# Rotating block-made queries and keys: halves swapped by ScalarE copies and three whole VectorE operations, and a slot of its own for the sample tile's keys

## The chip, the cores and the metric

The kernel runs on one core of one Trainium2 chip. The metric is the time of one execution on the device in microseconds (us), as a median over runs. A core has engines that run side by side, each through its own list of instructions in order: TensorE (PE; loads of stationary operands are shown apart as PEld), VectorE (DVE), ScalarE (ACT), GpSimd (POOL) and SyncE (SP), which issues the transfers (DMA). An instruction may wait for a semaphore of another engine or transfer; then everything behind it on its engine waits too. Tiles live in on-chip memory (SBUF, 128 partitions) or in the accumulators of TensorE (PSUM).

## The reference, cut to what matters

One layer over a prompt of 2048 frames and 8 running streams of 16 new frames each. The input projection makes retention queries and keys (4 heads of 128), their values and gates, and sliding-window queries (8 heads of 64), keys and values (2 heads). Queries and keys are rotated:

```
def rope(x, pos, rot_dim, theta):
    ...
    xr = x[..., :rot_dim].astype(jnp.float32)
    x1, x2 = xr[..., :half], xr[..., half:]
    rot = jnp.concatenate([x1 * cos - x2 * sin, x2 * cos + x1 * sin], axis=-1).astype(x.dtype)
    return jnp.concatenate([rot, x[..., rot_dim:]], axis=-1)

def in_proj(x, pos, w_in):
    ...
    rq = rope(rq.reshape(b, t, RET_HEADS, RET_DK), pos, RET_DK, RET_THETA)
    rk = rope(rk.reshape(b, t, RET_HEADS, RET_DK) * (RET_DK ** -0.5), pos, RET_DK, RET_THETA)
    ...
    sq = rope(sq.reshape(b, t, SWA_HEADS, SWA_HD), pos, SWA_ROT_DIM, SWA_THETA)
    sk = rope(sk.reshape(b, t, SWA_KV_HEADS, SWA_HD), pos, SWA_ROT_DIM, SWA_THETA)
```

For retention the whole head of 128 is rotated, in halves of 64; for the sliding window only the first 16 of 64. Then come chunkwise retention and banded attention with sinks, an output projection, layer norm, an MLP (1024 to 4096 to 1024, squared ReLU) and a second layer norm. The sliding-window keys of the last 128 prompt frames and of the 128 new frames are outputs as well.

## The kernel before, in words

The 2176 frames are 17 tiles of 128: 0 to 15 are the prompt, 16 (`SAMPLE`) holds the new frames of the eight streams. They are worked through in three groups, `[0..4]`, `[5..10]` and `[16, 11..15]`. A group passes through stages, whose names stand in the tile names of the profile: `1kv` is keys and values of the sliding window in group 1 (counted from 0), `1qk` retention queries and keys, `1sq` sliding-window queries and their attention, `1ret` retention, `1out` the output projection, `1mlp` the MLP.

The order of the instructions on each engine is fixed when the program is built. A planner (`Sched`) keeps a modelled clock for each engine; side work is written as tasks (Python generators) that yield the modelled time at which they want to go on. Between each three matmuls (`mm3`) the planner lets those tasks run whose time has come (`S.pump`); where TensorE needs a result, `finish` and `S.until` run tasks until it is there. `idle()` holds a task back while VectorE's modelled backlog is over 1 us. So an operation that is modelled shorter, or put on another engine, moves others around it. Transfers are all issued by SyncE in the order in which the tasks ask for them (but for a few on GpSimd).

Tiles come from pools by tag, with a fixed number of slots: `y` has 20, `u3` 8, `xT` 14, `st` 2, and in PSUM `mm` 2, `rt` 2, `sw` 4. `take` gives out the slot that was freed first, and what writes it first waits for the last reader of its former tile, be that an engine or a transfer.

In groups 1 and 2 the retention queries and keys are made by blocks: for each head h seven products (`QK`: 11, 12, S2, S1, S4, S3, 22) of 12 matmuls of 384 frames each stand in for eight (`qk_units`). S3 and 22 of a head share a PSUM bank. ScalarE copies products to `y` tiles of 128x384 (`keep`, `direct`), VectorE adds others to them from PSUM (`plus`); TensorE can only start product 22 of a head when `plus` has read S3 of it. A finished block, transposed (dimension on the partitions, frames along the row), goes to `rope_task`, which multiplies it by a table of cosines and sines and leaves it in `xT`. There are 16 blocks a group: 4 heads, queries and keys (u), two halves of the group's frames (v). The table of a half v (`table`, 384 KB, in a `u3` slot) is loaded when the first block asks for it. In the profile a rotation reads `xT_2qk<-y_2qk,u_2qk` for the halves, `y_2qk<-y_2qk,u_2qk` for the cosine and `xT_2qk<-xT_2qk,y_2qk` for the sum, all in line 310, the helper `vtt`; line 294 is ScalarE's copy (`acopy`), 316 a fused operation of VectorE (`vstt`), 275 a matmul, 281 a transpose on TensorE, 356 a transfer's issue.

The sliding-window keys of a tile (`kv_task`) are copied from PSUM by ScalarE into a tile of the pool `y` (groups 1 and 2), rotated by a few small VectorE operations (`rope_small`), for tiles 15 and 16 written out by a transfer, and transposed by TensorE. `sq_task` does the like for queries.

Of the kernel before, what the change touches and what calls it, by code (L numbers as in the profile page):

```python
# [11 lines left out]
ALU = mybir.AluOpType  # L12
AX = mybir.AxisListType

P = 128
# [3 lines left out]
SAMPLE = 16  # L19
# [157 lines left out]
def tile_layer(ctx: ExitStack, tc: tile.TileContext, A: dict, O: dict):  # L177
# [6 lines left out]
    S = Sched()  # L184
# [10 lines left out]
    def room(tag, n=1):  # L195
        return live[tag] + n <= CAP[tag]
# [5 lines left out]
    def take(tag, shape, dt=F32):  # L202
        if not room(tag):
            assert not S.inside, f"no room in {tag}"
            S.until(lambda: room(tag))
        live[tag] += 1
        cnt[0] += 1
        t = (psp if tag in PS else sb).tile(shape, dt, tag=tag, bufs=CAP[tag], name=f"{tag}_{ph[0]}_{cnt[0]}")
        name = t.tensor.name if hasattr(t, "tensor") else t.name
        tag_of[name] = tag  # L210
        S.fence[name] = min(freed[tag])
        freed[tag].remove(S.fence[name])
        return t
# [18 lines left out]
    def drop(*tiles):  # L232
        for t in tiles:
            name = t.tensor.name if hasattr(t, "tensor") else t.name
            mine = [u for u in lent if u.tensor.name == name]
            if mine:
                i = (t.offset % DM) // 512
                spare_blocks.append(mine[0][:, 512 * i:512 * i + 512])
                continue
            tag = tag_of.pop(name)  # L240
            live[tag] -= 1
            freed[tag].append(S.last(name) + S.ALIEN)
            for tab in (S.wr, S.rd):
                tab.pop(name, None)

    def wait_room(tag, n=1):
        while not room(tag, n):
            yield S.now + 0.3
# [6 lines left out]
    def size(ap):  # L255
        n = 1
        for d in ap.shape[1:]:
            n *= d
        return n
# [18 lines left out]
    def transpose(out, in_):  # L278
        cost = 0.110 + (0.2 if S.parts != (False, False) else 0.0)
        S.parts = (False, False)  # L280
        S.run("PE", lambda: nc.tensor.transpose(out, in_, ident), [out], [in_], cost)
# [11 lines left out]
    def acopy(out, in_):  # L293
        S.run("ACT", lambda: nc.scalar.copy(out, in_), [out], [in_], 0.06 + 0.83e-3 * size(out))  # L294

    def dcost(out):
        return 0.067 + 1.04e-3 * size(out)
# [4 lines left out]
    def copy(out, in_):  # L302

        n = size(out)
        ta = S.start_of("ACT", [out], [in_]) + 0.06 + 0.83e-3 * n
        tv = S.start_of("DVE", [out], [in_]) + dcost(out) + 0.3
        (acopy if ta <= tv else vcopy)(out, in_)

    def vtt(out, a, b, op):
        S.run("DVE", lambda: nc.vector.tensor_tensor(out, a, b, op), [out], [a, b], dcost(out))  # L310
# [37 lines left out]
    def dma(out, in_):  # L348
        t = S.start_of("SP", [out], [in_])
        S.free["SP"] = t + 0.06  # L350
        on_chip = out if hasattr(out.tensor, "slot_key") else in_
        nbytes = on_chip.shape[0] * size(on_chip) * 4
        end = max(S.free["DMA"], t + 1.1) + nbytes / 359e3
        S.free["DMA"] = end
        S.note("DMA", [out], [in_], end + 1.0)
        nc.sync.dma_start(out=out, in_=in_)
# [455 lines left out]
    def idle(eng="DVE", slack=SLACK):  # L812
        while S.free[eng] > S.now + slack:
            yield S.now + 0.2
# [238 lines left out]
    def rope_small(x, nh, t, ab):  # L1053

        c = cst[:, C_RS + 16 * t:C_RS + 16 * t + 8]
        s = cst[:, C_RS + 16 * t + 8:C_RS + 16 * t + 16]
        xv = x[:, :, 0:16].rearrange("p h (u f) -> p h u f", u=2)
        a = ab[:, 0:16 * nh].rearrange("p (h u f) -> p h u f", u=2, f=8)
        b = ab[:, 16 * nh:32 * nh].rearrange("p (h u f) -> p h u f", u=2, f=8)
        vtt(a, xv, c.unsqueeze(1).unsqueeze(1).broadcast_to([P, nh, 2, 8]), ALU.mult)  # L1060
        vtt(b, xv, s.unsqueeze(1).unsqueeze(1).broadcast_to([P, nh, 2, 8]), ALU.mult)
        vtt(xv[:, :, 0, :], a[:, :, 0, :], b[:, :, 1, :], ALU.subtract)
        vtt(xv[:, :, 1, :], a[:, :, 1, :], b[:, :, 0, :], ALU.add)

    def kv_task(t, si, ps, kTall, vall):
        tag = "y" if ph[0][0] != "0" else "xT"
        yield from wait_room(tag)
        kb = take(tag, [P, 256])
        krf = kb[:, 0:P]
        kr = krf.rearrange("p (g d) -> p g d", g=2)  # L1070
        acopy(krf, ps[:, 0:P])
        acopy(vall[:, si, :], ps[:, P:2 * P])
        drop(ps)
        yield S.ready(krf, eng="DVE")
        rope_small(kr, 2, t, kb[:, P:2 * P])
        if t >= NT - 2:
            nm = "p" if t == NT - 2 else "s"
            yield S.ready(krf, eng="SP")
            dma(O["swa_k_" + nm], krf)
            dma(O["swa_v_" + nm], vall[:, si, :])  # L1080
        yield S.soon(krf, more={'0': 0.0}.get(ph[0][0], 3.0))
        yield from wait_room("rt")
        tp = take("rt", [P, P])
        transpose(tp, krf)
        drop(kb)
        copy(kTall[:, (si) * P:(si + 1) * P], tp)
        drop(tp)
# [730 lines left out]
    for gi, tiles in enumerate(GROUPS):  # L1818
# [12 lines left out]
        def table(v):  # L1831
            while v not in tables:
                yield from wait_room("u3")
                if v in tables:
                    break
                tables[v] = t = take("u3", [P, 2, 384])
                dma(t, A["ropeT"][gi - 1, v])
                tabled[v] = 0
            return tables[v]
# [3 lines left out]
        def rope_task(c, h, u, v):  # L1843

            tab = yield from table(v)
            if h not in qkT:
                while h not in qkT and not room("xT"):
                    yield S.now + 0.3
                if h not in qkT:
                    qkT[h] = take("xT", [P, 1536])  # L1850
            dst = qkT[h][:, 768 * u + 384 * v:768 * u + 384 * v + 384]
            yield S.ready(c, tab, eng="DVE")
            yield from idle()
            vtt(dst[0:64], c[64:128], tab[64:128, 1, :], ALU.mult)
            vtt(dst[64:128], c[0:64], tab[0:64, 1, :], ALU.mult)
            yield from idle()
            vtt(c, c, tab[:, 0, :], ALU.mult)
            vtt(dst, dst, c, ALU.add)
            drop(c)
            tabled[v] += 1  # L1860
            if tabled[v] == 2 * RH:
                drop(tables[v])

        def qk_units(gi):

            def rope(c, h, u, v):
                rope_tasks[h, v].append(S.add(rope_task(c, h, u, v)))
# [105 lines left out]
        if gi:  # L1973
            T, used, qkT = {}, {}, {}
# [6 lines left out]
        for tis, kts in [(a, [0]), (a, [1]), (a, [2]), (a, [3]), (b, [0, 1, 2, 3]), (a, [4, 5]), (a, [6, 7]),  # L1981
# [9 lines left out]
            for ti in tis:  # L1991
# [3 lines left out]
                for kt in kts:  # L1995
                    o = P * (ti % 3)
                    xh, xl = x_at(gi, ti // 3, kt, slice(o, o + P))
                    c = (kt % 4) * 256
# [110 lines left out]
        for ui, u in enumerate(units):  # L2109
            nh, ti = u  # L2110
            t = tiles[ti]
# [406 lines left out]
```

## Time and profile before

| what | value |
|---|---|
| median of 3 runs | 2274.81 us (2274.16 to 2275.93) |
| profiled execution, its own time | 2276.4 us |
| its span (first to last instruction) | 2274.6 us |
| granted TensorE clock, mean | 0.997 of full |
| busy: PE, PEld, DVE, ACT, POOL | 2245.1, 1978.4, 1616.5, 925.7, 73.3 us |

How the lines are read that follow. A row of a timeline has the start (us from the start of the span), the duration, the engine, the source line, the operation, what it writes and reads by the program's names, the shape, how many are put together (x), and in brackets how long the engine had stood idle before it and what ended that. SPq is SyncE's own queue: a transfer's issue, not the transfer. A row of the waits has the waiting instruction, the releaser, us in total, times, the longest. A row of windows has the stretch, its length, then busy time and instructions of each engine, the granted clock, the busy share of the transfer engines and GB/s. A row of groups has busy us, mean ns of one, then the idle time ahead of it and what ended it.

### The profile page before, as it was taken

Reading aid. Unit: us, or ns where it says so; the run is one execution under the profiler, and the core shown is the slowest. Engines: PE = TensorE matmul, PEld = TensorE weight load, DVE = VectorE, ACT = ScalarE, POOL = GpSimd, SP = SyncE. Lnnn points to the kernel's source line nnn. Section 1 sums busy time; section 2 is a strip of 40 time slices with the busy share of each in tenths; the row PEclk is TensorE's granted clock in tenths of the full one; section 3 lists DMA queues with packets and bytes.
Section 4 is the critical chain, followed back from the end, with each engine's and each line's share of the span. In section 5 each row is a group of like instructions: output and inputs, shape, how many; then the busy total and the mean of one; then the engine's idle time right before and its main releaser. Section 6 shows DMA issues by size and latency. Waiting matters only on the chain. (4 is left out here: it accounts for less than half of the span.)

```text
span 2274.6 us, 34114 instructions
## 1 busy us (share of the span) xinstructions
PE 2245.1 (99%) x12185; PEld 1978.4 (87%) x12185; DVE 1616.5 (71%) x3472; ACT 925.7 (41%) x2205; POOL 73.3 (3%) x104
## 2 busy tenths in 40 slices
PE   9999999999999999999999999999999999999998
PEld 7788899998889878889989899898778899999987
DVE  6766788788878877788766666798654865555557
ACT  5534644444454255474233333252433732222222
POOL 0000000000000000000000000000010000000002
PEclk9999999999999999999999999999999999999999
DMA  7646746787899767759999999984344577777776
GB/s 277 210 167 230 274 177 236 262 287 277 280 335 376 241 231 254 270 189 359 360 374 368 372 353 357 347 311 183 129 138 166 175 251 258 252 256 252 250 257 180
DMA packets 205976, 598.34 MB, mean 263 GB/s; under 512 B 21872, under 2 KB 54384, under 8 KB 205808
## 3 DMA queue, kind: packets, MB, share of 16 engines
q1 hardware_dynamic: 204512, 593.81, 72.7%
q0 software_dynamic: 1296, 2.36, 0.6%
q8 instruction: 96, 1.57, 0.3%
q14 instruction: 72, 0.59, 0.1%
HBM read 422.48 MB, written 171.18 MB: 261 GB/s over the span
## 5 line engine op out<-in xcount | busy, mean ns | idle before, releaser
L275 PE MATMUL sw_2mlp<-xT_2out,w_2mlp 128*128 128x384 f32 x1152 | 209.0, 335 | 0.3 <-DVE kvln_2mlp L310 0.3
L275 PE MATMUL sw_1mlp<-xT_1out,w_1mlp 128*128 128x384 f32 x1152 | 209.1, 335 | 0.0
L275 PEld LDWEIGHTS sw_2mlp<-xT_2out,w_2mlp 128*128 128x128 f32 x1152 | 202.1, 188 | 4.2 <-DVE kvln_2mlp L310 0.6
L275 PEld LDWEIGHTS sw_1mlp<-xT_1out,w_1mlp 128*128 128x128 f32 x1152 | 202.3, 188 | 3.7
L275 PE MATMUL sw_0mlp<-xT_0out,w_0mlp 128*128 128x320 f32 x1188 | 180.2, 309 | 1.8 <-ACT y_0mlp L294 1.4
L275 PEld LDWEIGHTS sw_0mlp<-xT_0out,w_0mlp 128*128 128x128 f32 x1188 | 176.5, 188 | 5.0 <-ACT y_0mlp L294 1.8
L275 PE MATMUL rt_1mlp<-w_1mlp,u_1mlp 128*128 128x512 f32 x516 | 127.3, 391 | 1.2 <-DMA w_1mlp<-keptd 1.1
L275 PE MATMUL rt_2mlp<-w_2mlp,u_2mlp 128*128 128x512 f32 (+1 forms) x522 | 127.1, 388 | 0.0
L275 PE MATMUL rt_0mlp<-w_0mlp,u_0mlp 128*128 128x512 f32 x492 | 122.5, 394 | 1.6 <-ACT w_0mlp L294 0.8
L275 PE MATMUL mm_2mlp<-w_2mlp,u_2mlp 128*128 128x512 f32 (+1 forms) x504 | 122.5, 388 | 0.0
L275 PE MATMUL mm_1mlp<-w_1mlp,u_1mlp 128*128 128x512 f32 x492 | 121.6, 391 | 0.8 <-DMA w_1mlp<-keptd 0.8
L275 PEld LDWEIGHTS rt_1mlp<-w_1mlp,u_1mlp 128*128 128x128 f32 x516 | 96.3, 188 | 21.2 <-DMA w_1mlp<-keptd 2.2
L275 PEld LDWEIGHTS rt_2mlp<-w_2mlp,u_2mlp 128*128 128x128 f32 x522 | 96.9, 188 | 19.0
L275 PE MATMUL mm_0mlp<-w_0mlp,u_0mlp 128*128 128x512 f32 x456 | 111.6, 390 | 1.7 <-ACT w_0mlp L294 0.9
L275 PEld LDWEIGHTS rt_0mlp<-w_0mlp,u_0mlp 128*128 128x128 f32 x492 | 92.6, 190 | 21.3 <-DVE w_0mlp L310 1.3
L275 PEld LDWEIGHTS mm_2mlp<-w_2mlp,u_2mlp 128*128 128x128 f32 x504 | 93.6, 188 | 18.4
L275 PEld LDWEIGHTS mm_1mlp<-w_1mlp,u_1mlp 128*128 128x128 f32 x492 | 91.8, 188 | 19.5 <-DMA w_1mlp<-keptd 1.4
L275 PEld LDWEIGHTS mm_0mlp<-w_0mlp,u_0mlp 128*128 128x128 f32 x456 | 85.0, 188 | 19.4 <-ACT w_0mlp L294 1.4
L310 DVE TENSOR_TENSOR w_0mlp<-raw_0mlp,w_0mlp 128x512 fp32r<-128x512 f32 (+1 forms) x70 | 64.7, 925 | 44.7 <-ACT w_0mlp L294 30.4
L310 DVE TENSOR_TENSOR w_1mlp<-w_1mlp,w_1mlp 128x512 fp32r<-128x512 f32 (+1 forms) x100 | 67.2, 687 | 20.5 <-ACT w_1mlp L294 15.4
L294 ACT CAST u_2mlp<-kvln_2mlp 128x384 fp32r<-128x384 f32 x51 | 26.2, 515 | 117.7 <-PE mm_2mlp L275 44.1
L294 ACT CAST w_1mlp<-w_1mlp 128x512 fp32r<-128x512 f32 x70 | 43.4, 620 | 71.8 <-PE sw_1mlp L275 24.1
(974 smaller groups left out, 4713.5 us busy)
## 6 DMA issues: line engine op xcount, KB each, us to landing
w_1mlp<-keptd SPq DMA_DIRECT2D x112, 512.0 KB, 7.1
w_1mlp<-kept SPq DMA_DIRECT2D x104, 512.0 KB, 6.0
w_2mlp<-kept SPq DMA_DIRECT2D x104, 512.0 KB, 4.0
w_2mlp<-keptd SPq DMA_DIRECT2D x98, 512.0 KB, 4.1
kept<-w_0mlp SPq DMA_DIRECT2D x96, 512.0 KB, 3.4
keptd<-w_1mlp SPq DMA_DIRECT2D x70, 512.0 KB, 6.1
raw_0mlp<-in_wdn_dram SPq DMA_DIRECT2D x31, 512.0 KB, 5.9
keptq<-y_0mlp SPq DMA_DIRECT2D x56, 256.0 KB, 3.7
```

The costliest lines, as they stand in the source:

```text
L275: S.run("PE", lambda: nc.tensor.matmul(out, lhsT, rhs, start=start, stop=stop, skip_group_check=again), [out], [lhsT, rhs], cost)
L294: S.run("ACT", lambda: nc.scalar.copy(out, in_), [out], [in_], 0.06 + 0.83e-3 * size(out))
L310: S.run("DVE", lambda: nc.vector.tensor_tensor(out, a, b, op), [out], [a, b], dcost(out))
```

## The change

A rotation was four VectorE operations: the two halves of 64 partitions each multiplied crosswise (upper half of the block by sine into the lower half of the result, and the reverse), the block by cosine, and the sum. Now ScalarE copies the halves crosswise into the result, and VectorE does three operations on all 128 partitions: block by cosine, result by sine, sum. The sign that belongs to the sine moves with it to the other half of the table, which the host lays out. The task now waits for its place in `xT` and for the block on ScalarE ahead of the copies, and holds back for VectorE's backlog only ahead of the multiplications (one `idle()` after the table, one ahead of the sum).

The second edit: the sample tile's keys are taken from the pool `st` where it has room, and else from `y` as before; the others stay.

```diff
     def kv_task(t, si, ps, kTall, vall):
         tag = "y" if ph[0][0] != "0" else "xT"
-        yield from wait_room(tag)
-        kb = take(tag, [P, 256])
+        while not room(tag) and not (t == SAMPLE and room("st")):
+            yield S.now + 0.3
+        kb = take("st" if t == SAMPLE and room("st") else tag, [P, 256])
...
             dst = qkT[h][:, 768 * u + 384 * v:768 * u + 384 * v + 384]
-            yield S.ready(c, tab, eng="DVE")
-            yield from idle()
-            vtt(dst[0:64], c[64:128], tab[64:128, 1, :], ALU.mult)
-            vtt(dst[64:128], c[0:64], tab[0:64, 1, :], ALU.mult)
+            yield max(S.ready(c, eng="ACT"), S.fence[qkT[h].tensor.name])
+            acopy(dst[0:64], c[64:128])
+            acopy(dst[64:128], c[0:64])
+            yield S.ready(c, tab, dst, eng="DVE")
             yield from idle()
             vtt(c, c, tab[:, 0, :], ALU.mult)
+            vtt(dst, dst, tab[:, 1, :], ALU.mult)
+            yield from idle()
             vtt(dst, dst, c, ALU.add)
...
-    ropeT = np.concatenate([rt, rt * np.array([1.0, -1.0], np.float32)[:, None]], 2)
+    ropeT = np.concatenate([rt * np.array([1.0, -1.0], np.float32)[:, None], rt], 2)
```

The order of instructions differs from stage `1qk` to `1out` and from `2kv` to `2out`; the rest of the program stands as it was. VectorE has 36 instructions fewer (64 halves, 32 wholes more, and 4 copies less), ScalarE 68 more (64 copies of halves, and 4 copies which the planner moved there); TensorE has the same ones. Three places follow. A number behind a name only tells tiles apart; `DMAHW...` in a wait is a transfer's semaphore.

ScalarE in the stage `2kv` before: between the squares for the layer norm of group 1 stand the copies of keys out of PSUM.

```order
L290 ACTIVATE y_2kv_15428,tiny_2kv_15387<-y_1out_10492,tiny_2kv_15386 128x512 [waits Activation_49]
L294 COPY y_2kv_15464<-sw_2kv_15409 128x128 [waits DMAHW4_49,PE_49]
L294 COPY kvln_2kv_15372<-sw_2kv_15409 128x128
L294 COPY kvln_2kv_15371<-rt_2kv_15510 128x128 [waits PE_49]
L290 ACTIVATE y_2kv_15495,tiny_2kv_15457<-y_1out_10405,tiny_2kv_15456 128x512 [waits DVE_49]
```

After, the same place:

```order
L290 ACTIVATE y_2kv_15445,tiny_2kv_15404<-y_1out_10509,tiny_2kv_15403 128x512 [waits Activation_49]
L294 COPY y_2kv_15481<-sw_2kv_15426 128x128 [waits PE_49]
L294 COPY kvln_2kv_15389<-sw_2kv_15426 128x128
L294 COPY kvln_2kv_15388<-rt_2kv_15527 128x128 [waits PE_49]
L290 ACTIVATE y_2kv_15488,tiny_2kv_15439<-y_1out_10310,tiny_2kv_15438 128x512 [waits DVE_49]
```

The copies stand in the same order; the first no longer waits for a transfer.

VectorE in the stage `2qk` before, from the last output sums of group 1 (line 316) to the second `plus` behind the second table (`u_2qk_15997` is that table, `mm_2qk_16047` and `mm_2qk_16070` are S3 of heads 0 and 1).

```order
L316 SCALAR_TENSOR_TENSOR y_1out_10797<-y_1out_10797,tiny_2qk_15871,y_1mlp_15269 128x512 [waits DVE_49]
L310 TENSOR_TENSOR xT_2qk_15723<-y_2qk_15995,u_2qk_15997 64x384 [waits DMAHW6_49,Activation_49]
L310 TENSOR_TENSOR xT_2qk_15723<-y_2qk_15995,u_2qk_15997 64x384
L310 TENSOR_TENSOR y_2qk_15995<-y_2qk_15995,u_2qk_15997 128x384 [waits DMAHW7_49,DVE_49]
L310 TENSOR_TENSOR xT_2qk_15723<-xT_2qk_15723,y_2qk_15995 128x384 [waits DVE_49]
L310 TENSOR_TENSOR xT_2qk_15752<-y_2qk_16017,u_2qk_15997 64x384 [waits Activation_49]
L310 TENSOR_TENSOR xT_2qk_15752<-y_2qk_16017,u_2qk_15997 64x384
L310 TENSOR_TENSOR y_2qk_15911<-y_2qk_15911,mm_2qk_16047 128x384 [waits DMAHW1_49,PE_49]
L310 TENSOR_TENSOR y_2qk_16017<-y_2qk_16017,u_2qk_15997 128x384 [waits DMAHW1_49,DVE_49]
L310 TENSOR_TENSOR xT_2qk_15752<-xT_2qk_15752,y_2qk_16017 128x384 [waits DVE_49]
L310 TENSOR_TENSOR y_2qk_15929<-y_2qk_15929,mm_2qk_16070 128x384 [waits PE_49]
```

After (`u_2qk_16023` is the table, `mm_2qk_16074` and `mm_2qk_16095` are S3 of heads 0 and 1):

```order
L316 SCALAR_TENSOR_TENSOR y_1out_10814<-y_1out_10814,tiny_2qk_15890,y_1mlp_15286 128x512 [waits DVE_49]
L310 TENSOR_TENSOR y_2qk_15934<-y_2qk_15934,mm_2qk_16074 128x384 [waits PE_49]
L310 TENSOR_TENSOR y_2qk_16021<-y_2qk_16021,u_2qk_16023 128x384 [waits DMAHW1_49,DMAHW0_49,Activation_49]
L310 TENSOR_TENSOR xT_2qk_15740<-xT_2qk_15740,u_2qk_16023 128x384
L310 TENSOR_TENSOR xT_2qk_15740<-xT_2qk_15740,y_2qk_16021 128x384 [waits DVE_49]
L310 TENSOR_TENSOR y_2qk_16044<-y_2qk_16044,u_2qk_16023 128x384 [waits Activation_49]
L310 TENSOR_TENSOR xT_2qk_15771<-xT_2qk_15771,u_2qk_16023 128x384
L310 TENSOR_TENSOR xT_2qk_15771<-xT_2qk_15771,y_2qk_16044 128x384 [waits DVE_49]
L310 TENSOR_TENSOR y_2qk_15954<-y_2qk_15954,mm_2qk_16095 128x384 [waits DMAHW2_49,PE_49]
```

`plus` of head 0 moved from behind the first use of the table to ahead of it; `plus` of head 1 now stands behind two whole rotations. On SyncE's queue the table's load stands behind two more stores of output tiles than before.

VectorE in the stage `1sq` before, from the first rotation of sliding-window queries (`xT_1sq` and `u_1sq`) on; `st_1sq`, `raw_1sq` are parts of weights.

```order
L310 TENSOR_TENSOR xT_1sq_8526<-u_1sq_8510,cst 128x128 [waits Activation_49]
...
L310 TENSOR_TENSOR raw_1sq_8469<-raw_1sq_8470,raw_1sq_8469 128x512 [waits DVE_49]
L310 TENSOR_TENSOR xT_1qk_8056<-y_1qk_8120,u_1qk_8037 64x384 x2
L310 TENSOR_TENSOR y_1qk_8120<-y_1qk_8120,u_1qk_8037 128x384 [waits DVE_49]
L310 TENSOR_TENSOR xT_1qk_8056<-xT_1qk_8056,y_1qk_8120 128x384 [waits DVE_49]
L310 TENSOR_TENSOR y_1qk_8136<-y_1qk_8136,u_1qk_8037 128x384
L310 TENSOR_TENSOR xT_1qk_8073<-xT_1qk_8073,y_1qk_8136 128x384 [waits DVE_49]
L310 TENSOR_TENSOR xT_1sq_8579<-u_1sq_8561,cst 128x128 [waits Activation_49]
```

After:

```order
L310 TENSOR_TENSOR xT_1qk_8095<-xT_1qk_8095,y_1qk_8171 128x384 [waits DVE_49]
L310 TENSOR_TENSOR xT_1sq_8552<-u_1sq_8539,cst 128x128 [waits Activation_49]
...
L310 TENSOR_TENSOR raw_1sq_8494<-raw_1sq_8495,raw_1sq_8494 128x512 [waits DVE_49]
L310 TENSOR_TENSOR raw_1sq_8583<-raw_1sq_8494,raw_1sq_8583 128x512 [waits Activation_49]
L310 TENSOR_TENSOR xT_1sq_8606<-u_1sq_8590,cst 128x128 [waits Activation_49]
```

All rotations of retention blocks now stand ahead of the first of the sliding-window queries.

## The prediction, made before the changed kernel had run

> **What bounds the kernel now.** I read the page's busy times first, then TensorE's waits over the whole span, then busy times by stage, and last the instructions around each wait.
>
> ```profile
> span 2274.6 us, 34114 instructions
> PE 2245.1 (99%) x12185; PEld 1978.4 (87%) x12185; DVE 1616.5 (71%) x3472; ACT 925.7 (41%) x2205; POOL 73.3 (3%) x104
> ```
>
> TensorE (PE) is busy for 2245.1 of 2274.6 us. No edit touches a matmul, so all that can be won lies in the 29.5 us in which it stands still, and in what its clock loses. VectorE (DVE) at 71% is no bound over the span; it can be one only in a stage. The view of waits, TensorE alone, the rows that fall in the stages whose order the change moves:
>
> ```profile
> PE mm_2qk L275 <- DVE y_2qk L310: 2.2, 1, 2.2
> PE rt_2qk L281 <- ACT kvln_2kv L294: 1.9, 1, 1.9
> PE rt_2ret L275 <- DMA u_2ret<-in_st_dram: 1.6, 1, 1.6
> PE sw_1sq L275 <- ACT y_1sq L294: 1.6, 1, 1.6
> PE sw_1sq L281 <- DVE u_1sq L310: 1.5, 2, 1.3
> PE rt_2sq L281 <- DVE u_2sq L310: 1.3, 2, 0.7
> ```
>
> Columns: total, times, longest. These six make 10.1 us. That is the whole stock for a change that shortens VectorE's work here, plus what the clock loses. The busy times by stage (PE, PEld, DVE, ACT, POOL, granted clock, DMA) show how tight VectorE is there: group 1's queries and keys, then its sliding-window queries, then group 2's keys, and its queries and keys:
>
> ```profile
> 715.00:775.00 60.00, 60.00 (x343) 59.26 (x342) 41.97 (x72) 14.82 (x27) 0.00 (x0) 1.00 0.92 325
> 775.00:830.00 55.00, 51.55 (x296) 40.43 (x295) 46.03 (x118) 28.19 (x89) 0.00 (x0) 1.00 0.62 236
> 1480.00:1500.00 20.00, 18.12 (x134) 17.76 (x134) 15.88 (x52) 12.83 (x44) 1.10 (x2) 1.00 0.99 374
> 1500.00:1560.00 60.00, 57.83 (x319) 56.73 (x318) 56.54 (x109) 20.74 (x47) 3.58 (x4) 0.97 0.88 325
> ```
>
> In 1500 to 1560 VectorE is busy for 56.54 of 60 us, as full as TensorE, and ScalarE (ACT) for 20.74. That is the stage where fewer VectorE operations count, and the only one of the four with a clock under 1.00.
>
> **Part 1: the sample tile's keys in their own slot.** The timeline at the key-and-value stage of group 2:
>
> ```profile
> 1494.61 0.27 ACT L294 COPY y_2kv<-sw_2kv 128x128 f32<-128x128 f32 x1 [6.31 <-DMA out_swa_k_s_dram<-y_2kv]
> 1494.91 0.30 DVE L310 TENSOR_TENSOR y_2kv<-y_2kv,cst 128x32 f32<-128x32 f32 x2 [2.19 <-ACT y_2kv L294]
> 1498.85 0.33 PE L281 MATMUL rt_2qk<-cst,y_2kv 128*128 128x128 f32 x1 [1.88 <-ACT kvln_2kv L294]
> ```
>
> ScalarE's next key copy goes into the slot from which the sample keys are being written out, and stands 6.31 us for that transfer. What is queued behind it (two copies, two squares with their sums, more key copies) comes late, and TensorE's transpose waits 1.88 us for one of those copies. In the new order the copy waits for its matmul alone. Gain: 1.9 us at most. At least 0: if a square's inputs (VectorE's 2.19 us of waiting ends with this copy, not before it) were as late anyway. I take 1.9, since all of ScalarE's backlog there is this one wait. The change takes no room from anything: the other keys keep their tiles.
>
> **Part 2: the price of a rotation.** The rows around the second table of group 2 (start, duration):
>
> ```profile
> 1533.97 0.45 SPq L356 DMA_DIRECT2D u_2qk<-in_ropeT_dram  x1
> 1541.63 1.12 DVE L310 TENSOR_TENSOR xT_2qk<-y_2qk,u_2qk 64x384 f32<-64x384 f32 x2 [1.92 <-DMA u_2qk<-in_ropeT_dram]
> 1542.79 0.56 DVE L310 TENSOR_TENSOR y_2qk<-y_2qk,u_2qk 128x384 f32<-128x384 f32 x1
> 1543.95 1.12 DVE L310 TENSOR_TENSOR xT_2qk<-y_2qk,u_2qk 64x384 f32<-64x384 f32 x2
> 1545.11 0.56 DVE L310 TENSOR_TENSOR y_2qk<-y_2qk,mm_2qk 128x384 f32<-128x384 f32 x1
> 1545.58 0.55 DVE L310 TENSOR_TENSOR y_2qk<-y_2qk,u_2qk 128x384 f32<-128x384 f32 x1
> 1545.72 5.99 PE L275 MATMUL mm_2qk<-xT_2qk,w_2qk 128*128 128x384 f32 x24 [2.17 <-DVE y_2qk L310]
> 1546.16 0.56 DVE L310 TENSOR_TENSOR xT_2qk<-xT_2qk,y_2qk 128x384 f32<-128x384 f32 x1
> 1551.55 4.32 PE L275 MATMUL rt_2qk<-xT_2qk,w_2qk 128*128 128x384 f32 x24
> ```
>
> One rotation takes 1543.95 − 1541.63 = 2.32 us: two half operations that cost as much as whole ones, and two whole ones. Whole operations start 0.47 us apart where the second does not need the first (1545.11 to 1545.58) and 0.58 where it does (1545.58 to 1546.16). Three whole ones therefore take between 0.47 + 0.58 + 0.47 = 1.53 and 3 × 0.58 = 1.74 us; I take 1.64, the middle, so 0.68 us less for each, 11 us in each group of 16.
>
> The Trainium skill (VectorE: DVE Perf Modes, section "Two Vector instructions with no wait between them") says that an instruction starting in another group of 32 partitions than the input or output before it is held until all earlier ones have finished. By that rule the crossing halves could never overlap and the whole ones can: 1.53, and 13 us in a group; the trace agrees for the halves, with 1.12 us for two.
>
> The two copies go to ScalarE. No row shows one of 64x384; the nearest are these, by operation:
>
> ```profile
> L294 ACT COPY y_2qk<-sw_2qk 128x384 f32<-128x384 f32 x16 | 7.7, 481 | 15.3 <-DMA out_y_dram<-y_1out 8.3 <-DMA out_y_dram<-y_1ret 2.8 <-PE sw_2qk L275 2.6
> L294 ACT CAST u_2mlp<-kvln_2mlp 128x384 fp32r<-128x384 f32 x51 | 26.2, 515 | 117.7 <-PE mm_2mlp L275 44.1 <-PE rt_2mlp L275 42.6 <-DVE kvln_2mlp L310 12.0
> L310 DVE TENSOR_TENSOR xT_2qk<-y_2qk,u_2qk 64x384 f32<-64x384 f32 x32 | 17.7, 553 | 2.5 <-DMA u_2qk<-in_ropeT_dram 1.9
> ```
>
> At 0.48 to 0.52 us the 32 copies of a group make 15.4 to 16.6 us. ScalarE works 14.8 of 60 us in group 1's stage and 20.7 of 60 in group 2's, so they fit beside TensorE: cost 0 at the end. What could uncover them is ScalarE's wait for a late output transfer (the 8.3 us in the first of these rows): a copy queued behind that comes late to VectorE, by microseconds; but a rotation has its data long before its table, so I price it at 0 to 1 and take 0.
>
> **Part 3: the wait for the second table (group 2, queries and keys).** TensorE's last products (22 of heads 0, 1, then 2, 3) need PSUM banks that VectorE empties with "plus". Plus of head 0 started at 1545.11, behind two halves, whole, add, two halves, all behind the table that landed 7.66 us after its issue at 1533.97. TensorE had been free since 1545.72 − 2.17 = 1543.55. The loss is more than the wait: from 1545.72 to 1551.55 are 5.83 us for 24 matmuls, and the next 24 of the same shape take 4.32. The granted clock:
>
> ```profile
> 1497.00:1499.00 2.00, 0.15 (x2) 0.15 (x2) 1.90 (x8) 1.97 (x8) 0.55 (x1) 1.00 0.87 326
> 1545.00:1547.00 2.00, 1.28 (x5) 1.28 (x6) 1.93 (x5) 0.00 (x0) 0.00 (x0) 0.79 1.01 406
> 1547.00:1549.00 2.00, 2.00 (x8) 2.00 (x7) 1.89 (x5) 0.00 (x0) 0.00 (x0) 0.50 1.05 418
> 1549.00:1551.00 2.00, 2.00 (x11) 2.00 (x11) 1.96 (x4) 0.00 (x0) 0.00 (x0) 0.86 1.01 407
> ```
>
> So the stall costs 2.17 + 5.83 − 4.32 = 3.7 us. The 1.88 us of idle at 1497 left the clock at 1.00, so I expect a shorter stall to cost only itself.
>
> In the new order plus of head 0 stands ahead of the table's first use: it can run before 1541.6 and its wait is gone. Next in line is head 1, whose plus stands behind two rotations: 1541.63 + 2 × 1.64 + 0.56 = 1545.5, against a need at 1543.55 + 2.16 = 1545.7: just in time. Head 2's stands behind two more multiplications and a third rotation: 1545.5 − 0.1 + 1.64 + 2 × 0.47 + 0.56 = 1548.5, against 1547.9: 0.6 late. Its table's load now stands behind two more output stores on SyncE (SP), each of which waits for a VectorE operation of some 0.7 us; VectorE is ahead by what part 1 freed, so I add 0 to 1.2 and take 0.4. Residue 1.0; gain 2.7, between 0 (the table comes later by as much as is won) and 3.7.
>
> The Trainium skill (TensorE: Matmul & The Clock Gate, section "What's actually happening") has the clock halve after an idle window of about 3.4 us. By that rule 2.17 us of waiting could not have done it, and the slow stretch would stay: the sum would be 5.83 − 4.32 = 1.5 us less. The trace does not agree with that reading: the only slow stretch here begins with the longest wait.
>
> **Part 4: group 1's sliding-window queries.** Here VectorE drags a backlog of rotations along from group 1's second table, which landed at 755.54:
>
> ```profile
> 755.54 1.12 DVE L310 TENSOR_TENSOR xT_1qk<-y_1qk,u_1qk 64x384 f32<-64x384 f32 x2 [6.28 <-DMA u_1qk<-in_ropeT_dram]
> 783.05 0.49 DVE L310 TENSOR_TENSOR xT_1sq<-u_1sq,cst 128x128 f32<-128x128 f32 x2
> 784.09 0.63 PE L281 MATMUL rt_1sq<-cst,u_1sq 128*128 128x128 f32 x4 [0.39 <-DVE u_1sq L310]
> 784.47 1.64 PE L275 MATMUL mm_1sq<-w_1qk,xT_0mlp 128*128 128x512 f32 x6
> 787.66 1.57 PE L275 MATMUL sw_1sq<-kvln_1kv,y_1sq 64*128 64x192 f32 x16 [1.55 <-ACT y_1sq L294]
> 797.92 1.12 DVE L310 TENSOR_TENSOR xT_1qk<-y_1qk,u_1qk 64x384 f32<-64x384 f32 x2
> 801.25 0.30 PE L281 MATMUL sw_1sq<-cst,u_1sq 128*128 128x128 f32 x1 [1.34 <-DVE u_1sq L310]
> ```
>
> Of the 12 rotations that were open at 755.54, ten pairs of halves start before 783.05 and the wholes of nine are done; the rest is strewn in behind, the last pair at 797.92. In the new order all stand ahead of the first small rotation (783.05). They take 12 × 1.64 = 19.7 us instead of 9.5 × 2.32 = 22.0, so this operation comes 2.3 us earlier, at 780.7; with the one behind it, it is through within a microsecond, at 781.6. TensorE's transpose could start at 784.09 − 0.39 = 783.7; it now stands six matmuls earlier, 1.6 us by the row at 784.47, and is due at 782.1. That wait is covered by some 0.5 us. The copy behind the 1.55 us had its turn after VectorE work that stood behind the same backlog, and the transposes at 801.25 stood behind the last rotation, begun at 797.92. All of 3.45 us (55 − 51.55 in the table) can go; at worst none does, as the planner moves TensorE's demands earlier too. I take 2.5, since the one margin that I can work out is under 1 us.
>
> **Part 5: the rest.** In group 2's sliding-window queries 1.3 us of waits for small rotations: the transposes stand three matmuls earlier and six later than before, with VectorE ahead; I take 1.0 of it. The wait for the sample states:
>
> ```profile
> 1673.60 1.00 SPq L356 DMA_DIRECT2D u_2ret<-in_st_dram  x2
> 1676.69 1.62 PE L275 MATMUL rt_2ret<-u_2ret,u_2ret 128*64 128x128 f32 x16 [1.60 <-DMA u_2ret<-in_st_dram]
> ```
>
> stays: the load is issued as late against its use as before. Every stage up to the output projections is planned anew, and the six rows above show what such an order leaves: single waits of 0.4 to 2.2. I charge 1.0 for one more of them.
>
> **Sum.** 1.9 + 2.7 + 2.5 + 1.0 − 1.0 = 7.1 us. The profiled execution took 2276.4 (span 2274.6 and 1.8 around it), 1.6 above the median 2274.81. 2276.4 − 7.1 = 2269.3 for it, and 2267.7 for the median.
>
> **Rivals.**
> *Only the slot pays.* The table's transfer, not VectorE, sets when the rotations end; it is issued as late, lands as late, and TensorE waits for head 1 or 2 what it waited for head 0, at the half clock again. For it: 1.92 us of VectorE's idle ended by the table itself. Against it: plus of head 0 no longer stands behind it. Then 1.9 and some 1.5 in group 1: 2271.4, within the 0.2% (4.5 us) that a measurement of this kernel can tell from no change.
> *All waits go.* 1.9 + 3.7 + 3.45 + 1.3 + 1.6 = 12.0: 2262.8. Against it: the margins above, and the states' load, which no part speeds up.
> *Slower: sample states behind cache loads.* In the order of group 2's retention the states of the third head stand on SP's queue behind the loads of the second half of the sample cache (six transfers; issues cost 0.5 each by the row at 1673.60, so 3 us a head). If heads 3 and 4 each find them 3 us later than the 1.60 now, 6 us are lost and 7.1 − 6 is left: no change. It turns slower by over 0.2% only from (7.1 + 4.5) / 2 = 5.8 us a head on, when the clock falls too, as it did after 2.17 us: some 2280. For it: this is the one row where TensorE waits for a transfer. Against it: TensorE's use moves back with the heads in the planner's order.
>
> **How the numbers follow.** My forecast (gain of 4.5 to 10) 0.54; all waits go (10 to 13) 0.10; only the slot pays, or new waits eat the rest (gain 0 to 4.5) 0.27; the same with a loss within 0.2% 0.04; slower 0.05. Faster by over 0.2%: 0.64; within: 0.31; slower: 0.05. The range leaves out the lowest tenth and the slower cases: from 2263 (a gain of 11.8) to 2274.5 (almost none).
>
> **What would show it.** Right: no ScalarE wait on the sample keys' transfer and no TensorE wait on group 2's key copies; rotations 1.5 to 1.75 us apart; VectorE some 18 us less busy (64 × 0.553 − 32 × 0.56), ScalarE 31 to 33 more; the clock at 1.00 around the second table; under 1.5 us idle in group 1's sliding-window queries. Wrong: a TensorE wait over 2 us for plus with a half clock behind it, or new waits over 3 us from group 1's output stage or group 2's retention.

## The result, and the profile after

| | before | after |
|---|---|---|
| median | 2274.70 us (6 runs) | 2263.72 us (6 runs) |
| ratio | | 0.9949, 95% interval 0.9937 to 0.9960 |
| profiled execution, span | 2276.4, 2274.6 | 2265.9, 2263.8 |

The change made the kernel 11.0 us faster by the medians. That is inside the range, but 4 us beyond the forecast of 2267.7. A gain of 11.0 belongs to the rival in which all waits go (2262.8, a gain of 10 to 13, chance 0.10) and not to my forecast (a gain of 4.5 to 10, chance 0.54). The page of the changed kernel, span and busy times:

```profile
span 2263.8 us, 34152 instructions
PE 2240.9 (99%) x12185; PEld 1975.3 (87%) x12185; DVE 1591.3 (70%) x3436; ACT 960.3 (42%) x2273; POOL 73.7 (3%) x104
```

VectorE is 25.2 us less busy, ScalarE 34.6 us more (the 64 copies of halves make 32.8 of it, the four copies that moved from VectorE the better part of the rest). TensorE's waits after the change, the rows that fall in the stages planned anew:

```profile
PE mm_1ret L275 <- DMA w_1sq<-halves_vg: 0.7, 1, 0.7
PE sw_1sq L275 <- ACT y_1sq L294: 0.5, 1, 0.5
PE rt_2ret L275 <- ACT xT_2ret L290: 0.2, 1, 0.2
```

1.4 us in three rows stand in the place of the 10.1 us in six. The stock was a little larger than the prediction says: two more rows of before fall in these stages, which makes 11.0 us.

```profile
PE mm_1out L275 <- DMA w_1out<-halves_out: 0.5, 1, 0.5
PE rt_1sq L281 <- DVE u_1sq L310: 0.4, 1, 0.4
```

The busy times by stage, the same four stretches as before (PE, PEld, DVE, ACT, POOL, granted clock):

```profile
715.00:775.00 60.00, 60.00 (x341) 59.03 (x340) 38.72 (x72) 30.76 (x58) 0.00 (x0) 1.00 0.93 324
775.00:830.00 55.00, 53.83 (x320) 43.10 (x319) 40.07 (x114) 31.39 (x98) 0.53 (x1) 1.00 0.71 263
1480.00:1500.00 20.00, 20.00 (x138) 19.89 (x138) 19.20 (x60) 16.84 (x51) 2.84 (x4) 1.00 1.01 371
1500.00:1560.00 60.00, 60.00 (x330) 57.34 (x330) 53.61 (x109) 32.31 (x67) 1.72 (x2) 1.00 0.85 307
```

In 1500 to 1560 TensorE now works without a gap at full clock, with ScalarE at half load. The timeline there: the table's issue and landing, the first rotations, plus of heads 0 to 2 (1531.74, 1538.47, 1541.41), TensorE's products S3 of heads 0 and 1 (1529.46) and its last products:

```profile
1526.48 0.70 SPq L356 DMA_DIRECT2D u_2qk<-in_ropeT_dram  x1
1529.46 4.32 PE L275 MATMUL mm_2qk<-xT_2qk,w_2qk 128*128 128x384 f32 x24
1531.74 0.56 DVE L310 TENSOR_TENSOR y_2qk<-y_2qk,mm_2qk 128x384 f32<-128x384 f32 x1 [2.54 <-PE mm_2qk L275]
1535.41 0.56 DVE L310 TENSOR_TENSOR y_2qk<-y_2qk,u_2qk 128x384 f32<-128x384 f32 x1 [3.11 <-DMA u_2qk<-in_ropeT_dram]
1535.88 0.55 DVE L310 TENSOR_TENSOR xT_2qk<-xT_2qk,u_2qk 128x384 f32<-128x384 f32 x1
1536.47 0.56 DVE L310 TENSOR_TENSOR xT_2qk<-xT_2qk,y_2qk 128x384 f32<-128x384 f32 x1
1536.94 0.55 DVE L310 TENSOR_TENSOR y_2qk<-y_2qk,u_2qk 128x384 f32<-128x384 f32 x1
1537.78 4.33 PE L275 MATMUL mm_2qk<-xT_2qk,w_2qk 128*128 128x384 f32 x24
1538.47 0.55 DVE L310 TENSOR_TENSOR y_2qk<-y_2qk,mm_2qk 128x384 f32<-128x384 f32 x1
1541.41 0.55 DVE L310 TENSOR_TENSOR y_2qk<-y_2qk,rt_2qk 128x384 f32<-128x384 f32 x1
1542.01 4.45 PE L275 MATMUL rt_2qk<-xT_2qk,w_2qk 128*128 128x384 f32 x24
```

A rotation takes 1535.41 to 1536.94, 1.53 us. VectorE now stands idle for 3.11 us before the table lands, and TensorE does not notice: plus of head 2 ends at 1541.96, and the products behind it start at 1542.01.

**Where the time came from.** The single times of one kernel spread by 4 to 9 us, and part of that is in stages that the change does not touch: stage 0mlp took 423.6 to 429.0 us over the profiles of all kernels here, though its instructions are the same. So I compare stages, each from TensorE's first instruction of it in the timeline to that of the next. The kernel before has three profiles (two taken later, below), the changed one two; the others one each. The labels are those of the experiments.

| us | 1kv to 1out | 2kv + 2qk | 2sq | 2ret | 2kv to 2out |
|---|---|---|---|---|---|
| before, 1st | 309.3 | 82.3 | 43.0 | 124.5 | 322.1 |
| before, 2nd | 308.8 | 80.4 | 42.9 | 124.6 | 320.1 |
| before, 3rd | 308.4 | 79.9 | 43.6 | 126.2 | 321.8 |
| changed, 1st | 305.5 | 76.4 | 40.9 | 123.9 | 313.6 |
| changed, 2nd | 306.0 | 76.2 | 40.9 | 123.9 | 313.4 |
| e1, slot alone | 308.0 | 78.3 | 43.7 | 126.2 | 320.4 |
| e2, rotation alone | 305.6 | 77.2 | 40.9 | 123.9 | 314.3 |
| e3, new order, old operations | 312.8 | 81.3 | 48.1 | 123.9 | 325.5 |
| e4, old order, new operations | 305.7 | 76.3 | 41.4 | 124.6 | 314.5 |
| e5, as e4, with the slot | 306.2 | 76.2 | 41.4 | 124.7 | 314.5 |
| e6, copies doubled | 306.9 | 76.2 | 40.9 | 123.9 | 313.4 |
| e7, before, table early | 308.2 | 82.4 | 42.6 | 123.9 | 321.2 |
| e8, changed, tables early | 307.0 | 76.2 | 40.9 | 124.1 | 313.6 |

By the means, group 1 gave 308.8 − 305.8 = 3.1 us and group 2 321.3 − 313.5 = 7.9, together 10.9 before rounding, close to the 11.0 of the medians. The spans of these profiles differ by 13.0 in the mean (2274.7 and 2261.8); the other 2 us lie in stages that the change does not touch, 0mlp above all. One of the 15 runs of the kernel before that were timed beside e1 to e4 took 5755.94 us and is left out of their ratios.

### The profile page after: what moved, and what is told of

The parts are those of the page before. It is cut to its first block, busy times and chain, and to the rows that moved or that the text cites. A ratio compares the mean times of both kernels' runs of the same rounds, so it can differ in the third digit from the quotient of the medians.

```text
span 2263.8 us, 34152 instructions
## 1 busy us (share of the span) xinstructions
PE 2240.9 (99%) x12185; PEld 1975.3 (87%) x12185; DVE 1591.3 (70%) x3436; ACT 960.3 (42%) x2273; POOL 73.7 (3%) x104
## 5 line engine op out<-in xcount | busy, mean ns | idle before, releaser
L310 DVE TENSOR_TENSOR w_0mlp<-raw_0mlp,w_0mlp 128x512 fp32r<-128x512 f32 (+1 forms) x70 | 64.7, 925 | 43.2 <-ACT w_0mlp L294 29.2
```

## The experiments

The edits are a rotation's operations, the planner's order and the keys' slot. The first four kernels take them apart. The ratios below are not those of the medians, and the us beside them are worked out from the ratio; between the medians it can be 1 us more or less. To hold the order in e3 and e4, the planner is told of the one set of operations (`S.run` takes an engine, what to issue, what is written and read, and a modelled cost) while the program issues the other; TensorE, SyncE and GpSimd then keep their order instruction for instruction.

### e1: the slot alone

The `kv_task` part of the diff on the kernel before, nothing else.

> The kernel before with the sample keys' own slot and nothing else; TensorE, SyncE and GpSimd keep the order of before. Theory (each wait is a thing by itself): ScalarE's 6.3 us and TensorE's 1.9 us in 2kv go; the wait for plus behind the second table of 2qk stays at 2 us or more, with the half clock; time 1 to 2.5 us under the kernel before. Rival (the stalls are one chain: TensorE comes earlier to the same late table): the wait for plus grows by 1.9 us and the time is that of before within 0.7 us.

Measured: 0.9994 of before (0.9985 to 1.0004), so −1.4 us, between −3.4 and +0.9: no gain that is clear of the spread (the medians are 2273.11 and 2273.15). TensorE's waits in group 2:

```profile
PE rt_2sq L281 <- DVE u_2sq L310: 1.9, 2, 1.3
PE rt_2ret L275 <- DMA u_2ret<-in_st_dram: 1.7, 2, 1.5
PE mm_2qk L275 <- DVE y_2qk L310: 0.9, 1, 0.9
PE rt_2qk L275 <- DVE y_2qk L310: 0.4, 1, 0.4
```

ScalarE's wait is gone and so is TensorE's 1.9, and the waits of 2sq and 2ret stay. Plus waits for 0.9 us, neither 2 or more as the theory had it nor longer as the rival had it, and the 24 matmuls behind it take 4.44 us, at full clock (1.00 over 1500 to 1560). The table's load was issued 2.6 us ahead of S3 of head 0 here (1528.26, S3 at 1530.87) and 1.1 to 1.4 ahead in the three profiles of before. So the theory, by which each wait is a thing by itself, does not hold, and neither does the rival's one chain.

### e2: the rotation alone

The changed kernel with the lines of `kv_task` as before.

> The changed kernel with all keys in the old pool, its order on TensorE and SyncE kept. Theory: ScalarE waits some 6 us for the sample keys' transfer again and TensorE 1.5 to 2.5 us behind it; all other waits of the old kernel stay away; 1.5 to 2.5 us over the changed kernel, 8 to 10 under the one before. Rival (VectorE's lead in 2qk came from the slot): VectorE is 3 us later, the second table and plus of heads 0 to 3 too, and 2 to 4 us more are lost there with a lower clock; 5 or more over the changed kernel.

Measured: 0.9965 (0.9952 to 0.9977), 8.0 us under before. ScalarE waits for the sample keys again, TensorE hardly. ScalarE's wait for their transfer, and TensorE's in 2qk:

```profile
ACT y_2kv L294 <- DMA out_swa_k_s_dram<-y_2kv: 4.7, 1, 4.7
PE rt_2qk L281 <- ACT kvln_2kv L294: 0.3, 1, 0.3
```

The rival (VectorE's lead came from the slot) is out as a loss of time: 2kv and 2qk take 77.2, against 76.2 to 76.4 with the slot. Its mechanism is there in part: the table's load is issued 1.4 us ahead of S3 of head 0 (1528.78, S3 at 1530.16) and 3.0 ahead with the slot, but TensorE does not wait for plus.

### e3: the new order with the old operations

```diff
-            acopy(dst[0:64], c[64:128])
-            acopy(dst[64:128], c[0:64])
+            for o, i in ((dst[0:64], c[64:128]), (dst[64:128], c[0:64])):
+                S.run("ACT", lambda: None, [o], [i], 0.06 + 0.83e-3 * size(o))
...
-            vtt(c, c, tab[:, 0, :], ALU.mult)
-            vtt(dst, dst, tab[:, 1, :], ALU.mult)
+            S.run("DVE", lambda: nc.vector.tensor_tensor(dst[0:64], c[64:128], tab[64:128, 1, :], ALU.mult), [c],
+                  [c, tab[:, 0, :]], dcost(c))
+            S.run("DVE", lambda: nc.vector.tensor_tensor(dst[64:128], c[0:64], tab[0:64, 1, :], ALU.mult), [dst],
+                  [dst, tab[:, 1, :]], dcost(dst))
+            nc.vector.tensor_tensor(c, c, tab[:, 0, :], ALU.mult)
```

The table has the sign of before.

> The changed kernel with its order on TensorE, SyncE and GpSimd and its slot, but each rotation done by the four VectorE operations of before and no ScalarE copy. Theory (VectorE's time decides): plus of heads 1 to 3 behind the second table come 0.5 to 3 us late, with the half clock, and the first small rotations of 1sq, behind twelve rotations of 2.32 us, 5 to 9 us late; 8 to 14 us over the changed kernel, so near the kernel before or slower. Rival (the order decides): under 2 us over the changed kernel.

Measured: 1.0044 (1.0031 to 1.0056), 10 us over before and some 20 over the changed kernel, more than either theory said. TensorE's waits in the stages planned anew, the longest five:

```profile
PE rt_1sq L281 <- DVE u_1sq L310: 5.4, 1, 5.4
PE rt_2sq L281 <- DVE u_2sq L310: 4.5, 1, 4.5
PE rt_2qk L275 <- DVE y_2qk L310: 2.1, 1, 2.1
PE mm_2qk L275 <- DVE y_2qk L310: 0.7, 1, 0.7
PE sw_1sq L275 <- ACT y_1sq L294: 0.5, 1, 0.5
```

The place of 1sq was named with 5 to 9 us and took 5.4; that of 2sq was not. The new order by itself is harmful: it puts all rotations ahead of work for which TensorE waits, and that only pays if they are short.

### e4: the old order with the new operations

```diff
-            vtt(dst[0:64], c[64:128], tab[64:128, 1, :], ALU.mult)
-            vtt(dst[64:128], c[0:64], tab[0:64, 1, :], ALU.mult)
+            for o, i, s in ((dst[0:64], c[64:128], tab[64:128, 1, :]), (dst[64:128], c[0:64], tab[0:64, 1, :])):
+                S.run("DVE", lambda: nc.scalar.copy(o, i), [o], [i, s], dcost(o))
...
+            nc.vector.tensor_tensor(dst, dst, tab[:, 1, :], ALU.mult)
             vtt(dst, dst, c, ALU.add)
```

The table has the sign of after.

> The kernel before with its order and its keys' slots, but each rotation done by two ScalarE copies and three whole VectorE operations. Theory (VectorE's time decides): the waits of 1sq (3.4 us) and 2sq (1.3) go but for 1 us, plus of head 0 behind the table comes 0.2 us late rather than 2.2, with full clock; the 1.9 us of 2kv stay; 6 to 8 us under the kernel before. Rival (the order decides): under 2 us below the kernel before.

Measured: 0.9964 (0.9952 to 0.9977), 8.2 us under before, with nothing moved on TensorE or SyncE. All its waits in the stages planned anew (1mlp, between them, has its waits for weights as in every profile here):

```profile
PE rt_2ret L275 <- DMA u_2ret<-in_st_dram: 1.7, 2, 1.6
PE sw_1sq L281 <- DVE u_1sq L310: 0.5, 2, 0.3
```

The theory of VectorE's time holds, and e3 and e4 together show it: with either order the new operations are the faster ones, by 8 us in the old and by some 20 in the new. The 1.9 us of 2kv are gone although the keys have their old slot.

### The changed kernel again, and e5: the old order with the new operations and the slot

e5 is e4 with the `kv_task` part of the diff.

> The changed kernel once more, beside the three others of this call on one chip: 10 to 13 us under the kernel before, with no TensorE wait over 0.6 us from 1kv to 2out but for transfers. Rival (its first lead held some luck): 8 to 9 us, like either half alone.

> The order of before on TensorE, SyncE and GpSimd, the new operations, and the sample keys' slot: all of the change but the new plan. Theory (the new order is worth nothing by itself): within 1.5 us of the changed kernel. Rival (the new order is worth what the whole change has over the new operations alone): 2 to 4 us over the changed kernel.

Measured on one chip: the changed kernel 0.9944 (0.9932 to 0.9956), 12.7 us under before, e5 0.9951 (0.9937 to 0.9965). The rival of some luck in the first lead is out. One wait of TensorE passed the 0.6 named, by little: 0.7 us in 1sq for a ScalarE copy. e5 is 0.8 us over the changed kernel by the medians, inside the theory's 1.5. By the table the new order is worth 314.5 − 313.5 = 1.0 us in group 2 (0.5 in 2sq and 0.8 in 2ret, less 0.1 each in 2qk and 2out) and nothing in group 1. The slot, e5 against e4, is worth 0.1 in 2kv and 2qk. The timed ratios alone can't tell e4, e5 and the changed kernel apart.

### e6: ScalarE's copies doubled

```diff
-            acopy(dst[0:64], c[64:128])
-            acopy(dst[64:128], c[0:64])
+            for o, i in ((dst[0:64], c[64:128]), (dst[64:128], c[0:64])):
+                S.run("ACT", lambda: [nc.scalar.copy(o, i) for _ in range(2)], [o], [i], 0.06 + 0.83e-3 * size(o))
```

> The changed kernel with each of the 64 ScalarE copies done twice, some 33 us more of ScalarE's time in the stages 1qk to 1sq and 2qk to 2sq; all orders kept. Theory (ScalarE's copies lie beside TensorE, and a block waits long for its table or for VectorE): within 1 us of the changed kernel. Rival (ScalarE's copies are on the path to the rotations and to PSUM banks): TensorE waits for ScalarE in 1qk or 2qk or for plus, 3 us or more over the changed kernel.

ScalarE's busy time, from the page:

```profile
PE 2242.4 (99%) x12185; PEld 1976.8 (87%) x12185; DVE 1591.7 (70%) x3436; ACT 992.0 (44%) x2337; POOL 74.2 (3%) x104
```

Measured: 0.9961 (0.9948 to 0.9975) against 0.9944 for the changed kernel on the same chip; the intervals overlap. 32 us more of ScalarE cost 1.0 us in group 1, where these two rows of waits stand, and nothing in group 2:

```profile
PE sw_1sq L275 <- ACT y_1sq L294: 2.0, 1, 2.0
PE rt_1sq L281 <- DVE u_1sq L310: 0.6, 1, 0.6
```

The medians are 4.1 us apart, more than the theory's 1 us and as much as the rival says, but not where the rival puts it: in the one profile the rest lies in stage 0mlp (427.2 us against 423.6), which stands ahead of all these copies. Whether it is chance stays open.

### e7: the kernel before with the second table of group 2 loaded early

```diff
                 dma(t, A["ropeT"][gi - 1, v])
                 tabled[v] = 0
+                if v == 0 and gi == 2:
+                    S.add(table(1))
```

> The kernel before with the second table of group 2 loaded with the first, 25 to 30 us earlier, which makes the planner order VectorE's work of 2qk and 2sq anew; old operations. Theory (the stall in 2qk was the table's transfer plus VectorE's rotations behind it): TensorE's wait for plus and the half clock go, 2 to 4 us under the kernel before, with the 3.4 us of waits of 1sq in place. Rival (VectorE, busy 56.5 of 60 us there, is what is short): the wait comes back at a later plus or in 2sq, and less than 1 us is gained.

Measured: 1.0002 (0.9993 to 1.0010). My theory fell. The timeline of 2qk: a fused sum on VectorE, the first pair of halves of the second table, plus of head 0, and TensorE's products:

```profile
1531.91 0.76 DVE L316 SCALAR_TENSOR_TENSOR y_1out<-y_1out,tiny_2qk,y_1mlp 128x512 f32<-128x512 f32 x1
1532.70 1.12 DVE L310 TENSOR_TENSOR xT_2qk<-y_2qk,u_2qk 64x384 f32<-64x384 f32 x2
...
1541.90 0.55 DVE L310 TENSOR_TENSOR y_2qk<-y_2qk,mm_2qk 128x384 f32<-128x384 f32 x1
...
1542.51 6.02 PE L275 MATMUL mm_2qk<-xT_2qk,w_2qk 128*128 128x384 f32 x24 [3.38 <-DVE y_2qk L310]
```

VectorE waits for no table and starts its rotations 2.1 us behind the start of S3 of head 0 (1530.64) instead of 6.6 as in the first profile of before, and TensorE waits longer, 3.38 us: the planner used the early table to put four rotations, 9.2 us, ahead of plus of head 0. From 1500 to 1560 VectorE is busy for 58.4 us and waits for nothing. With rotations of 2.32 us VectorE is what is short in this order; the table's landing was only the last thing that it waited for. What the early table would do in the old order, e7 does not show, since TensorE's order changed with it.

### The kernel before, twice more

> The kernel before, unchanged, for a second profile. If the two stalls of group 2 in its first profile are of the program: 1.9 us behind the key copy in 2kv, and about 2.2 us with half clock at plus in 2qk, so 64 to 65 us for the stage 2qk. If they hang on when transfers land in an execution: one or the other is smaller by a microsecond or more, and the stage shorter.

> The same once more, for a third profile: the same two cases.

TensorE's instruction behind the key copy and the products behind plus in the second profile, then in the third (the transpose of the second profile shows no wait):

```profile
1496.89 0.33 PE L281 MATMUL rt_2qk<-cst,y_2kv 128*128 128x128 f32 x1
1543.58 6.03 PE L275 MATMUL mm_2qk<-xT_2qk,w_2qk 128*128 128x384 f32 x24 [1.98 <-DVE y_2qk L310]
```

```profile
1498.51 0.33 PE L281 MATMUL rt_2qk<-cst,y_2kv 128*128 128x128 f32 x1 [0.35 <-ACT kvln_2kv L294]
1545.06 4.46 PE L275 MATMUL mm_2qk<-xT_2qk,w_2qk 128*128 128x384 f32 x24 [1.85 <-DVE y_2qk L310]
```

The wait for plus comes in every execution (2.17, 1.98, 1.85). The other stall does not: 1.88, 0 and 0.35 us. And the half clock behind plus came in two executions of three.

### e8: the changed kernel with both second tables early

The insertion of e7 without `and gi == 2`, on the changed kernel.

> The changed kernel with the second table of both groups loaded together with the first; TensorE's order is that of the changed kernel but for three matmuls. Theory (with the short rotations neither the table nor VectorE is on TensorE's path in 2qk): same time as the changed kernel within 1 us, while VectorE's wait of 3 us for the table goes. Rival (the table still limits, with margins of tenths): 1 to 2 us faster.

Measured: 0.9956 (0.9943 to 0.9970), so no faster than the changed kernel. VectorE's waits in 1500 to 1560:

```profile
DVE y_2qk L310 <- ACT xT_2qk L294: 1.9, 3, 0.6
DVE xT_2sq L310 <- ACT u_2sq L290: 1.8, 1, 1.8
```

The 3.1 us for the table are gone, 2kv and 2qk take 76.2 us as before that: neither table nor VectorE is on TensorE's path there any more. Group 1, whose second table is early too, takes 307.0 us, 1.2 more than in the changed kernel, with a wait of 1.5 us for a ScalarE copy in 1sq.

## Why the prediction fell short

The mechanism held: shorter rotations take VectorE off TensorE's path, beside copies that ScalarE hides. The sum of 7.1 us was 4 us too small, and its terms were mis-sized in both directions. Parts 1 and 3 together forecast 4.6 us for 2kv and 2qk, and by the means of the table these gave 4.5 (80.9 to 76.3). That fit is luck: I had read an execution in which both stalls were at the long end. The missing 4 us are 1.3 in 2sq and 1.2 in 2ret beyond what part 5 gave, the 1.0 that it charged, and 0.6 in group 1, less 0.1 in 2out.

- **Part 1, the slot, 1.9 us: not a term by itself.** I took one execution's wait for the program's. In the other two profiles of before it is 0 and 0.35: ScalarE's wait is 4.5 and 4.8 us there, not 6.31, and ends about when TensorE needs the copy. With the new operations the slot gives 0.1 (e5 against e4) to 0.9 us (changed against e2). With the old ones e1's one profile has more: 78.3 in 2kv and 2qk, against 79.9 to 82.3, since plus waits less. So slot and short rotations seem to save in part the same wait, and a sum of parts can count it twice.
- **Part 2, the price of a rotation: right**, at its lower end. 1.53 us, not my middle of 1.64. That is what the rule of the Trainium skill gave (VectorE: DVE Perf Modes, section "Two Vector instructions with no wait between them"), and the trace agrees. VectorE's busy time fell by 25.2, not 18. In the old order (e4) it is 1594.9, 21.6 less than before: operations that overlap count once, and I had subtracted durations. Most of the rest came with the new order (e3, with the old operations, has 1613.8, 2.7 less), in which four copies moved to ScalarE. ScalarE's copies of 64x384 took 0.51 each in the trace of after:

```profile
L294 ACT COPY xT_2qk<-y_2qk 64x384 f32<-64x384 f32 x32 | 16.4, 512 | 14.9 <-DVE y_2qk L310 14.5
```

  inside the bounds taken, and they cost little that one profile shows (e6: the same again costs 1.0 us).
- **Part 3, the second table of 2qk, 2.7 us: too small for the execution that I read.** 2kv and 2qk together lose 6.1, 4.2 and 3.6 us in the three profiles of before over the 76.2 that they take without waits, and all of it went. Two steps failed. "Head 2 0.6 late" came from 1.64 a rotation; three rotations at 1.53 are 0.33 us shorter. "0.4 for the table behind two more stores" had the wrong sign: the load was issued 2.98 us before S3 of head 0 (1526.48, S3 at 1529.46), not 1.09 before it as in the first profile of before, and though it then took 8.9 us to land and not 7.66, the table was there 0.6 us sooner against S3. The stores do cost: e5, in the old order, issues the load 4.9 us ahead of S3, 1.9 more than the changed kernel. But they wait for VectorE (SyncE's wait in 1505 to 1537 of after, first line), and the short rotations bring VectorE there sooner: with the old ones in the same order (e3, the next two lines) the load is issued 0.26 us behind S3, 3.2 us later. The slot adds 1.6 (e2). Plus of head 2 ended 0.05 us ahead of the need.

```profile
SPq L356 <- DVE y_1out L316: 8.3, 11, 2.0
```

```profile
1536.33 4.32 PE L275 MATMUL mm_2qk<-xT_2qk,w_2qk 128*128 128x384 f32 x24
1536.59 1.56 SPq L356 DMA_DIRECT2D u_2qk<-in_ropeT_dram  x1
```

  The rival "only the slot pays" saw the table as the bound. In e2 the table is in use 6.1 us behind the start of S3, nearly as late as before (6.6), and TensorE does not wait for plus; e8 takes VectorE's wait for the table away and gains nothing. So it was not.
- **Part 4, group 1's sliding-window queries, 2.5 us: about right**, 3.1 by the table. The first small rotation came at 778.13 instead of the 780.7 worked out, mostly because the table landed at 753.13 instead of 755.54 (stage 1kv began 1.4 us earlier in this execution). Counted from the landing it came after 25.0 us, where I had 25.2. The 1.3 us that 12 rotations at 1.53 instead of 1.64 save went into a wait that I had not seen, of VectorE for ScalarE:

```profile
769.58 0.96 DVE L310 TENSOR_TENSOR xT_1qk<-u_1qk,xT_1qk 128x768 fp32r<-128x768 f32 x1 [1.95 <-ACT xT_1qk L294]
```

- **Part 5: wrong twice.** 2sq gave 2.3 us, not 1.0 (43.2 to 40.9): e4 has 1.8 of it in the old order. The wait for the sample states went with the new order, 125.1 to 123.9 us in 2ret; e4 and e5, in the old order, keep it. The load is issued at 1671.32 and used at 1676.69 in the new order, 5.4 us ahead instead of 1.5 (1673.60, and the wait began at 1675.09). The new wait that I charged with 1.0 came: 0.7 for a weight in 1ret and the 0.2 in 2ret. The table's differences already hold it.
- **The slower rival** placed a loss at these loads. They did move back on SyncE's queue, but their use moved back more. A slower kernel was near in another place: e3's order with the old rotations.

## What to carry to other kernels

Where a stage's in-order engine is nearly as busy as the bound, price the change of its whole backlog (start to start, not duration), and follow it into the queues that wait for that engine: here the table's load came sooner because stores ahead of it waited for VectorE. A stall that the trace puts down to a transfer need not be that transfer's; loading it early, in the order that the planner then made, moved the wait and saved nothing. The gains of two edits that shorten the way to one wait need not add up: test each alone and both. And a wait of 1 or 2 us in one profile can be one execution's: a second profile of the kernel before would have shown which stalls come every time.

## What the runs showed of the hardware

A stall of 1.5 to 2 us sometimes halves TensorE's clock and sometimes does not. Behind plus, the same 24 matmuls took 6.03 us after a stall of 1.98 us and 4.46 after one of 1.85. Behind the sample states' load in 2ret, the second and third profile of before show the same stall; the timeline of the second, then of the third:

```profile
1674.41 0.40 PE L275 MATMUL rt_2ret<-u_2ret,u_2ret 128*64 128x128 f32 x2 [1.52 <-DMA u_2ret<-in_st_dram]
1676.01 1.13 PE L275 MATMUL sw_2ret<-u_2ret,xT_2ret 64*128 64x512 f32 x4
1677.06 1.20 PE L275 MATMUL sw_2ret<-u_2ret,y_2sq 64*64 64x144 f32 x16
```

```profile
1675.93 0.40 PE L275 MATMUL rt_2ret<-u_2ret,u_2ret 128*64 128x128 f32 x2 [1.55 <-DMA u_2ret<-in_st_dram]
1677.51 1.77 PE L275 MATMUL sw_2ret<-u_2ret,xT_2ret 64*128 64x512 f32 x4
1679.20 2.18 PE L275 MATMUL sw_2ret<-u_2ret,y_2sq 64*64 64x144 f32 x16
```

The matmuls that follow take 1.13 and 1.20 us in the one and 1.77 and 2.18 in the other, where the granted clock is 0.50 from 1678 to 1680. So the length of a stall alone does not decide, and my reading that 1.88 us is short enough and 2.17 too long was wrong. The Trainium skill (TensorE: Matmul & The Clock Gate, section "What's actually happening") says that the window of activity runs freely, so that it depends on the moment when the clock changes; these runs fit that, though a stall of about half its 3.4 us was enough here. Which moment it is, no run here shows.
